# The output product's rows on two fixed sets of buffers, one of them lent by the prompt attention

## The chip, the cores and the metric

One core of a Trainium2 chip (trn2) runs the whole program. The metric is device time in microseconds (us) of one execution, taken as the median of several; lower is better. The engines are TensorE (PE; its weight loads are listed as PEld), VectorE (DVE), ScalarE (ACT), GpSimd (POOL) and SyncE (SP, which issues most DMAs, in order).

## The reference

One inference step of a small decoder with model width 1024: one recurrent layer (RG-LRU), from whose output shared keys, values and forget gates are made, then one attention layer with forget gates. It runs over 2048 prompt tokens and over 64 decode tokens (8 sequences of 8, each with 4096 cached keys). The change touches the end of the attention layer, its output product:

```python
def fox_mixer(x, k, v, cq, ck, q_pos, k_pos, w_in, w_out):
    z = x @ w_in
    q, g = z[..., :D_ATTN], z[..., D_ATTN:]
    o = fox_attention(q, k, v, cq, ck, q_pos, k_pos).reshape(B, T, D_ATTN)
    return (o * jax.nn.silu(g)) @ w_out

y = fox_mixer(rms_norm(x, b_pre_norm[l]), k_all, v_all, cq, ck, q_pos, k_pos, b_w_in[l], b_w_out[l])
x = x + rms_norm(y, b_post_norm[l])
```

All data are 32-bit floats. The kernel keeps that precision in products by splitting each factor into a high part, rounded to the format that PE takes, and a low part (the rest), and adding three products: high by high, high by low, low by high.

## The kernel before

The program first runs the recurrent layer, then the projections for keys, values, queries and gates, with the decode attention woven in. Last comes the prompt attention, and after it the output product with its norm and residual.

**Prompt attention** (`attention`, L1309 on). 64 units run one after the other: 16 heads by 4 blocks of 512 queries (`qc`). An odd head takes the blocks in the order 3, 2, 1, 0, so the last unit is head 15, block 0. Per unit, for each tile of 128 keys, PE makes scores into one of two banks of PSUM, the accumulator memory (`st`, L1537 to L1540), ACT takes the exponential into a tile `p` or, for the first, `acc` (L1546), PE multiplies groups of four with the values (`ops`, L1557), and POOL adds the exponentials up (`acc`, L1563). After a unit ACT copies the two halves of `ops` (`oT`, `odd`, L1438 and L1442) and POOL adds them; PE sums the exponentials (`tot`, L1460), ACT copies that (`cs`), small DMAs turn it round (`sums`, `r`), DVE takes the reciprocal, PE spreads it over the rows (`rp`, L1484), POOL and DVE multiply (`sgt`), and the gated result goes to a DRAM tensor per query block (`og_d[qc]`, L1487). These steps behind a unit are put off by some ticks in a list (`later`); `later.flush()` at the end of `attention` issues what is left.

The attention's keys and values lie in tiles of their own for even and odd heads: `kbs[0]`, `vvs[0]` and one of the two buffers tagged `ka` belong to the even heads, the last of which is head 14.

**Output product** (`project`, L1599). There are 17 rows of work (L1581): row 0 the 64 decode tokens, rows 1 to 16 blocks of 128 prompt tokens from the last block to the first, so rows 1 to 4 read `og_d[3]` and rows 13 to 16 `og_d[0]`. Per row: load 512 KB of gated attention (`og`) and 512 KB of residual (`x1`), cast the high part on ACT (`oh`, L99) and subtract for the low part on DVE (`ol`, L106), 2 x 24 matmuls of 128 x 512 into two banks (`y`, L368 to L370), then `post`: the sums of squares on ACT (`junk`, L499), a reciprocal square root of some twelve small operations on DVE (`nr_...`, L226 to L236), a scaling on DVE that reads the banks (`yo`, L1637), the residual added on POOL (L106), and the store.

The rows run in two groups. Rows 0 to 2 (`EARLY = 3`) use a pool `proje` with one buffer of each kind and two PSUM banks that the decode attention had (`psum["dec"]`, tags `d` and `o`). For rows 3 to 16 the attention's pools are closed, and a second pool, `proj`, with two buffers of each kind, and six PSUM banks (four of them for `y`) are opened on their memory.

The order of the instructions on each engine is not the order of the code: a scheduler takes, by its own estimates, the earliest instruction in the code that is ready, and places waits for data and for buffers. Each engine then runs its list in that order.

Of the kernel before, what the change touches and what calls it, by code (L numbers as in the profile page):

```python
# [11 lines left out]
F32 = mybir.dt.float32  # L12
F32R = mybir.dt.float32r
# [7 lines left out]
P = 128  # L21
D = 1024
KB = 8
SEQ = 2048
# [23 lines left out]
ODD = "G"  # L48
RAMP = 8
NS = 3  # L50
EARLY = 3
SHARE0 = 2.0
LEFT = 16
AHEAD = 8
# [25 lines left out]
def f(ap):  # L80

    return ap.bitcast(F32)
# [3 lines left out]
def tile_hawk_fox(  # L86
# [120 lines left out]
    def sbuf(es, name, side=None):  # L207
        return es.enter_context(tc.tile_pool(name=name, bufs=1, side=side, reuse_waits="tile"))

    def banks(es, name, n):  # L210
        return es.enter_context(tc.tile_pool(name=name, bufs=n, space=PSUM, reuse_waits="tile"))

    psum = {}

    def mmp(name="mm"):
        return psum["mm"].tile([P, 512], F32, name=name, tag="mm", bufs=4)
# [142 lines left out]
    later = Later()  # L359
# [629 lines left out]
    def drain(gen):  # L989
        for _ in gen:  # L990
            pass
# [317 lines left out]
    def attention(es):  # L1309
        pool = sbuf(es, "att")  # L1310
        ps3 = psum["att"]
# [8 lines left out]
        vvs = [pool.tile([P, 16, HD], F32, name=f"vvt{i}") for i in range(2)]  # L1320
        pool.tile([P, SEQ], F32R, name="ka", tag="ka", bufs=2)
        kbs = [pool.tile([P, SEQ], F32R, name="kbt0")]
# [30 lines left out]
               ident[:16, 8 + h2 * 4:12 + h2 * 4].unsqueeze(2).to_broadcast([16, 4, HD]), ALU.add)  # L1353
        less = pool.tile([4, 4], F32, name="less")
        V.tensor_scalar(less[:, :], ident[:4, :4], -1.0, 0.0, op0=ALU.mult, op1=ALU.add)
        units = [(h, qc) for h in range(H) for qc in ((0, 1, 2, 3) if h % 2 == 0 else (3, 2, 1, 0))]
        heads, qas, mxs, oTs_, sgt = {}, {}, {}, {}, {}

# [170 lines left out]
        for u, (h, qc) in enumerate(units):  # L1529
            load_low(u + 2)  # L1530
            for k in range(nks[u]):
# [44 lines left out]
                if k + sum(nks[u - u % 4:u]) == 3 and h + 1 < H:  # L1576
                    load_head(h + 1)
                yield 4.1 * (512 - lo) * 0.42 + (done[0] - before) * 213
        later.flush()

    rows = [(NSAMP, None, x1s_d[:, :], ys_flat)]  # L1581
    rows += [(P, t, x1_d[t:t + P], yp_flat[t:t + P]) for t in range(SEQ - P, -1, -P)]
    proj = {}
# [15 lines left out]
    def project(es):  # L1599

        bpostB, out = proj["g"], proj["out"]
        pool, nb = sbuf(es, "proje", "right"), 1
        raws, lds, xs = {}, {}, {}

        def load(i):
            if i >= lim:
                return
            m, t, res, _ = rows[i]
            og = pool.tile([P, KB, P], F32, name="ogT", tag="ogT", bufs=nb)
            if t is None:  # L1610
                tt(V, og[:, :, :m], oTs[:, :, :], sgs[:, :, :], ALU.mult)
            else:
                S.dma_start(og[:, :, :], og_d[t // 512][:, t % 512:t % 512 + P].rearrange("(k p) t -> p k t", p=P))
            x1 = pool.tile([P, D], F32, name="x1", tag="x1", bufs=nb)
            S.dma_start(x1[:m, :], res)
            raws[i], xs[i] = og, x1

        def split(i):
            if i >= lim:
                return  # L1620
            m = rows[i][0]
            og = raws.pop(i)
            oh = pool.tile([P, KB, P], F32R, name="ohT", tag="ohT", bufs=nb)
            ol = pool.tile([P, KB, P], F32R, name="olT", tag="olT", bufs=nb)
            cp(A, oh[:, :, :m], og[:, :, :m])
            tt(V, ol[:, :, :m], og[:, :, :m], f(oh[:, :, :m]), ALU.subtract)
            lds[i] = oh, ol

        def post(i, yps):
            m, t, res, dst = rows[i]  # L1630
            x1 = xs.pop(i)
            y = pool.tile([P, D], F32, name="yo", tag="yo", bufs=nb)
            ss = sumsq(pool, yps, m)
            r = rsqrt(ss[:m], m, 0.25 / D, post=0.5)
            for j in range(2):
                sl = slice(j * 512, (j + 1) * 512)
                V.scalar_tensor_tensor(y[:m, sl], yps[j][:m, :], r[:m, 0:1], bpostB[:m, sl], op0=ALU.mult, op1=ALU.mult)  # L1637
                tt(V if i == len(rows) - 1 and j == 1 else G, y[:m, sl], y[:m, sl], x1[:m, sl], ALU.add)
                if i == len(rows) - 1:
                    S.dma_start(dst[:, sl], y[:m, sl])  # L1640
            if i < len(rows) - 1:
                S.dma_start(dst, y[:m, :])

        for first, lim in ((0, EARLY), (EARLY, len(rows))):
            if first:
                yield
                pool, nb = sbuf(es, "proj"), 2
            for i in range(first, first + nb):
                load(i)
            split(first)  # L1650
            load(first + nb)
            for i in range(first, lim):
                yps = []
                for j in range(2):
                    ps = mmp("y") if first else psum["dec"].tile([P, 512], F32, name="y", tag="do"[j], bufs=1)
                    out.product(ps, rows[i][0], j, *lds[i])
                    yps.append(ps)
                    if j == 0 and nb > 1:
                        split(i + 1)
                post(i, yps)  # L1660
                if nb == 1:
                    split(i + 1)
                load(i + nb + 1)


    a_in = [[(0, a_w_in[0, :, n * P:(n + 1) * P]), (P, a_w_in[0, :, D + n * P:D + (n + 1) * P])] for n in range(KB)]
# [128 lines left out]
    psum["att"] = banks(att, "psa", 6)  # L1795
    side.along(attention(att), share)
    side.upto(1e12)
    pj = project(last)
    next(pj)
    att.close()  # L1800
    psum["mm"] = banks(last, "mm2", 6)
    drain(pj)
    last.close()


# [33 lines left out]
```

## Time and profile before

| | |
|---|---|
| median of 3 runs | 3090.72 us (3088.16 to 3099.72) |
| profiled execution, first to last instruction | 3081.2 us |
| mean granted clock of TensorE in it | 0.965 |
| PE busy | 2825.8 us (92%), 20462 instructions |
| DVE busy | 1805.6 us (59%) |
| ACT busy | 1295.0 us (42%) |
| POOL busy | 1155.5 us (38%) |
| first product of row 1 starts | 2864.39 us |
| last product of row 16 ends | 3071.80 us |

The profile is of one execution, and its times count from that execution's first instruction. A row of the timeline gives start, duration, engine, source line, operation, the tile written, the tiles read, shapes, count, and in brackets how long the engine had been idle and what ended the wait. SPq rows are DMA issues on SyncE's queue; what they show is the issue, not the transfer. A row of the busy times by stretch gives the stretch's start and end, its length, and then for each engine busy us with the number of instructions, the granted TensorE clock (1.00 is full), the busy share of the DMA engines and GB/s.

### The profile page before, as it was taken

What the parts mean: (1) busy time and instruction counts of PE and PEld (TensorE: products, weight loads), DVE (VectorE), ACT (ScalarE), POOL (GpSimd) and SP (SyncE); (2) the same over time, 40 slices, a digit from 0 to 9 for tenths busy, and PEclk for the clock granted to TensorE, in tenths of its full rate; (3) what the DMA queues carried; (4) which work ended last, traced back from release to release, by engine and by line L of the source; (5) the groups of instructions that cost most, each with busy time, mean ns of one, the idle gap of its engine ahead of it and who ended that gap; (6) DMA issues with size and microseconds to landing.
All of it is one profiled execution on the core that took longest, in us unless ns stands there. A gap on an engine that the chain in (4) does not pass through costs nothing.

```text
span 3081.2 us, 58151 instructions
## 1 busy us (share of the span) xinstructions
PE 2825.8 (92%) x20462; PEld 2177.5 (71%) x20462; DVE 1805.6 (59%) x4012; ACT 1295.0 (42%) x2874; POOL 1155.5 (38%) x1263
## 2 busy tenths in 40 slices
PE   6998999998999989997999799899999988999798
PEld 5997888988999978885797455455545554544587
DVE  7876555424367756755655666666667665543244
ACT  4665432232346655333333334444444445455211
POOL 1663101000025532000001456655656648788322
PEclk9999999999999999998999799999999999999899
DMA  4224547788622266999999998989999996331343
GB/s 121 89 76 150 154 137 216 242 267 254 198 84 86 79 195 198 327 305 315 325 331 307 292 303 261 289 268 321 289 294 314 317 295 211 97 87 41 96 135 111
DMA packets 492855, 653.25 MB, mean 212 GB/s; under 512 B 91100, under 2 KB 292829, under 8 KB 485286
## 3 DMA queue, kind: packets, MB, share of 16 engines
q1 hardware_dynamic: 488934, 643.87, 66.9%
q10 hardware_dynamic: 3340, 3.56, 0.4%
q8 instruction: 162, 2.65, 0.4%
q0 software_dynamic: 288, 2.10, 0.2%
q14 instruction: 131, 1.07, 0.1%
HBM read 513.82 MB, written 135.16 MB: 211 GB/s over the span
## 4 chain that ended last, share of the span: by engine, by line
PE 54%; DMA 20%; DVE 10%; ACT 5%; SPq 5%; issue 4%; POOL 2%; ACTq 0%; DVEq 0%; POOLq 0%
PE ops L1557 5%; DMA raw<-in_cache_k_dram 5%; PE y L368 4%; PE y L370 4%; PE y L369 4%; PE st L1537 3%; DMA raw<-in_cache_v_dram 3%; PE kv L369 3%; PE kv L368 3%; PE kv L370 3%; PE sx L1404 3%; PE dO L1237 2%; SPq L1074 2%; PE qg L368 2%; PE st L1538 2%
## 5 line engine op out<-in xcount | busy, mean ns | idle before, releaser
L106 POOL TENSOR_TENSOR acc<-acc,p 128x512 f32<-128x512 f32 (+3 forms) x576 | 638.8, 1109 | 291.7 <-PE ops L1557 226.4
L1546 ACT ACTIVATE p<-st 128x512 f32<-128x512 f32 (+3 forms) x576 | 290.4, 525 | 404.8 <-PE st L1538 188.6
L1159 DVE STREAM_TRANSPOSE ktr<-raw 128x1024 f32<-128x1024 f32 x256 | 305.4, 1223 | 161.3 <-DMA raw<-in_cache_k_dram 143.7
L1406 DVE TENSOR_REDUCE mxs<-sx 128x1 f32<-128x512 f32 x384 | 253.9, 680 | 143.5 <-PE sx L1404 142.5
L369 PE MATMUL kv<-wl,xh 128*128 128x256 f32 (+3 forms) x1088 | 309.1, 287 | 8.9 <-DVE wl L413 8.8
L368 PE MATMUL kv<-wh,xh 128*128 128x256 f32 (+3 forms) x1088 | 310.4, 290 | 5.7 <-ACT wh L412 5.3
L370 PE MATMUL kv<-wh,xl 128*128 128x256 f32 (+3 forms) x1088 | 309.2, 286 | 0.0
L1557 PE MATMUL ops<-p,vvt 128*64 128x512 f32 (+3 forms) x1152 | 292.7, 550 | 3.1 <-ACT p L1546 2.8
L1537 PE MATMUL st<-qa,ka 128*128 128x512 f32 (+3 forms) x640 | 273.3, 427 | 21.8 <-ACT p L1546 18.0
L1404 PE MATMUL sx<-kbt,qbt 96*128 96x512 f32 (+3 forms) x640 | 234.7, 426 | 26.1 <-DMA qbt<-qd 11.5
L1537 PEld LDWEIGHTS st<-qa,ka 128*128 128x128 f32 x640 | 123.6, 193 | 178.5 <-issue 112.1
L412 ACT ACTIVATE wh<-wst,gv 128x256 fp32r<-128x256 f32 (+1 forms) x384 | 164.4, 499 | 195.0 <-DMA wst<-in_b_w_in_dram 81.8
L1538 PE MATMUL st<-qbt,kbt 128*128 128x512 f32 (+3 forms) x640 | 237.0, 371 | 0.0
L413 DVE SCALAR_TENSOR_TENSOR wl<-wst,gv,wh 128x256 fp32r<-128x256 f32 (+1 forms) x384 | 169.9, 492 | 108.1 <-ACT wh L412 100.3
L368 PE MATMUL qg<-xh,wh 128*128 128x384 f32 (+2 forms) x640 | 229.1, 359 | 1.0 <-ACT wh L412 1.0
L370 PE MATMUL qg<-xh,wl 128*128 128x384 f32 (+2 forms) x640 | 227.5, 357 | 0.9 <-DVE wl L413 0.9
L369 PE MATMUL qg<-xl,wh 128*128 128x512 f32 (+2 forms) x640 | 226.9, 356 | 0.0
L1092 POOL TENSOR_TENSOR qw<-qb,amask 128x128 f32<-128x128 f32 x64 | 29.3, 465 | 498.8 <-PE dS L1127 258.0
L369 PEld LDWEIGHTS kv<-wl,xh 128*128 128x128 f32 (+1 forms) x1088 | 203.8, 188 | 12.7 <-DVE wl L413 10.4
L368 PEld LDWEIGHTS kv<-wh,xh 128*128 128x128 f32 (+1 forms) x1088 | 203.6, 189 | 11.8 <-ACT wh L412 6.0
L370 PEld LDWEIGHTS kv<-wh,xl 128*128 128x128 f32 (+1 forms) x1088 | 205.3, 189 | 3.9 <-issue 3.9
L1404 PEld LDWEIGHTS sx<-kbt,qbt 96*128 96x128 f32 x640 | 119.1, 203 | 94.4 <-DVE mxs L1406 25.1
(289 smaller groups left out, 6472.1 us busy)
## 6 DMA issues: line engine op xcount, KB each, us to landing
raw<-in_cache_k_dram SPq DMA_DIRECT2D x512, 256.0 KB
raw<-in_cache_v_dram SPq DMA_DIRECT2D x512, 256.0 KB
wst<-in_w_kv_dram SPq DMA_DIRECT2D x48, 512.0 KB
wst<-in_b_w_in_dram SPq DMA_DIRECT2D x48, 512.0 KB
xt<-in_x_prompt_dram SPq DMA_DIRECT2D x32, 512.0 KB
wst<-in_a_w_in_dram SPq DMA_DIRECT2D x64, 256.0 KB
x<-x SPq DMA_DIRECT2D x32, 512.0 KB
out_dram<-kf SPq DMA_DIRECT2D x128, 128.0 KB
```

Of the source, the lines that this page charges most:

```text
L106: eng.tensor_tensor(out, a, b, op=op)
L368: T.matmul(ps, lh(k), rh(k), start=(k == 0), stop=False)
L369: T.matmul(ps, lh(k), rl(k), start=False, stop=False)
L370: T.matmul(ps, ll(k), rh(k), start=False, stop=(k == nk - 1))
L413: V.scalar_tensor_tensor(wl[:, k, :], st[:, k, :], gk, f(wh[:, k, :]), op0=ALU.mult, op1=ALU.subtract)
L1159: V.transpose(t.kts[pp][:, n], raw[:, :, pp * 256:(pp + 1) * 256])
L1404: T.matmul(ps[:, :w], qb[0:96, j * P:(j + 1) * P], kb[0:96, ck * 512:ck * 512 + w], start=True, stop=True)
L1406: V.reduce_max(mx[:, j, ck:ck + 1], ps[:, :w], axis=AX.X)
L1537: T.matmul(ps[:, lo:], ka[:, ks], qa[:, lo:], start=True, stop=False)
L1538: T.matmul(ps[:, lo:], kb[:, ks], qb[:, lo:], start=False, stop=(k < qc * 4))
L1546: pair.append((k, lo, p, A.activation(p[:, lo:], ps[:, lo:], AF.Exp)))
L1557: return T.matmul(ops[r:r + HD, lo:], vvs[h % 2][:, k, :], p[:, lo:], start=(k < 2), stop=(last and k >= todo[-1][0] - 1))
```

## The change

Rows 0 to 16 all use two fixed sets of buffers in turn, row i the set i % 2. Set 0 is the pool `proje` and the two decode banks. Set 1 is lent by the attention through a dictionary: `og` and `x1` are the two halves of `kbs[0]`, `oh` and `ol` the two halves of a further tile with the tag `ka`, `y` is `vvs[0]`, and its PSUM banks are two further tiles with the tag `st`. The second pool and the six banks are gone. A row's load of `og` for row i + 2 and the split of row i + 1 are written behind the first half of row i's products, the load of the residual for row i + 2 behind row i's `post`. `later.flush()` moves from the end of `attention` to behind row 3. Lines of the changed kernel are up to two lower or higher than those of the kernel before; the operations themselves are the same.

```diff
--- before.py
+++ after.py
@@ -48,7 +48,6 @@
 ODD = "G"
 RAMP = 8
 NS = 3
-EARLY = 3
 SHARE0 = 2.0
 LEFT = 16
 AHEAD = 8
@@ -1353,6 +1352,8 @@
                ident[:16, 8 + h2 * 4:12 + h2 * 4].unsqueeze(2).to_broadcast([16, 4, HD]), ALU.add)
         less = pool.tile([4, 4], F32, name="less")
         V.tensor_scalar(less[:, :], ident[:4, :4], -1.0, 0.0, op0=ALU.mult, op1=ALU.add)
+        lent["psum"], lent["res"], lent["out"] = ps3, f(kbs[0][:, :]), vvs[0]
+        lent["halves"] = lambda: pool.tile([P, SEQ], F32R, name="ka", tag="ka", bufs=2)
         units = [(h, qc) for h in range(H) for qc in ((0, 1, 2, 3) if h % 2 == 0 else (3, 2, 1, 0))]
         heads, qas, mxs, oTs_, sgt = {}, {}, {}, {}, {}
 
@@ -1576,7 +1577,8 @@
                 if k + sum(nks[u - u % 4:u]) == 3 and h + 1 < H:
                     load_head(h + 1)
                 yield 4.1 * (512 - lo) * 0.42 + (done[0] - before) * 213
-        later.flush()
+
+    lent = {}
 
     rows = [(NSAMP, None, x1s_d[:, :], ys_flat)]
     rows += [(P, t, x1_d[t:t + P], yp_flat[t:t + P]) for t in range(SEQ - P, -1, -P)]
@@ -1599,37 +1601,28 @@
     def project(es):
 
         bpostB, out = proj["g"], proj["out"]
-        pool, nb = sbuf(es, "proje", "right"), 1
-        raws, lds, xs = {}, {}, {}
-
-        def load(i):
-            if i >= lim:
-                return
+
+        def tiled(t):
+            return t.rearrange("p (k t) -> p k t", k=KB)
+
+        def gated_rows(i, og):
             m, t, res, _ = rows[i]
-            og = pool.tile([P, KB, P], F32, name="ogT", tag="ogT", bufs=nb)
             if t is None:
                 tt(V, og[:, :, :m], oTs[:, :, :], sgs[:, :, :], ALU.mult)
             else:
                 S.dma_start(og[:, :, :], og_d[t // 512][:, t % 512:t % 512 + P].rearrange("(k p) t -> p k t", p=P))
-            x1 = pool.tile([P, D], F32, name="x1", tag="x1", bufs=nb)
+
+        def residual(i, x1):
+            m, t, res, _ = rows[i]
             S.dma_start(x1[:m, :], res)
-            raws[i], xs[i] = og, x1
-
-        def split(i):
-            if i >= lim:
-                return
+
+        def split(i, og, oh, ol):
             m = rows[i][0]
-            og = raws.pop(i)
-            oh = pool.tile([P, KB, P], F32R, name="ohT", tag="ohT", bufs=nb)
-            ol = pool.tile([P, KB, P], F32R, name="olT", tag="olT", bufs=nb)
             cp(A, oh[:, :, :m], og[:, :, :m])
             tt(V, ol[:, :, :m], og[:, :, :m], f(oh[:, :, :m]), ALU.subtract)
-            lds[i] = oh, ol
-
-        def post(i, yps):
+
+        def post(i, pool, yps, x1, y):
             m, t, res, dst = rows[i]
-            x1 = xs.pop(i)
-            y = pool.tile([P, D], F32, name="yo", tag="yo", bufs=nb)
             ss = sumsq(pool, yps, m)
             r = rsqrt(ss[:m], m, 0.25 / D, post=0.5)
             for j in range(2):
@@ -1641,26 +1634,38 @@
             if i < len(rows) - 1:
                 S.dma_start(dst, y[:m, :])
 
-        for first, lim in ((0, EARLY), (EARLY, len(rows))):
-            if first:
-                yield
-                pool, nb = sbuf(es, "proj"), 2
-            for i in range(first, first + nb):
-                load(i)
-            split(first)
-            load(first + nb)
-            for i in range(first, lim):
-                yps = []
-                for j in range(2):
-                    ps = mmp("y") if first else psum["dec"].tile([P, 512], F32, name="y", tag="do"[j], bufs=1)
-                    out.product(ps, rows[i][0], j, *lds[i])
-                    yps.append(ps)
-                    if j == 0 and nb > 1:
-                        split(i + 1)
-                post(i, yps)
-                if nb == 1:
-                    split(i + 1)
-                load(i + nb + 1)
+        pool = sbuf(es, "proje", "right")
+        hs = lent["halves"]()
+        sets = [dict(og=pool.tile([P, KB, P], F32, name="ogT"), x1=pool.tile([P, D], F32, name="x1"),
+                     oh=pool.tile([P, KB, P], F32R, name="ohT"), ol=pool.tile([P, KB, P], F32R, name="olT"),
+                     y=pool.tile([P, D], F32, name="yo"),
+                     ps=lambda j: psum["dec"].tile([P, 512], F32, name="y", tag="do"[j], bufs=1)),
+                dict(og=tiled(lent["res"][:, :D]), x1=lent["res"][:, D:], oh=tiled(hs[:, :D]), ol=tiled(hs[:, D:]),
+                     y=lent["out"][:, :, :].rearrange("p k d -> p (k d)"),
+                     ps=lambda j: lent["psum"].tile([P, 512], F32, name="y", tag="st", bufs=2))]
+
+        def part(i, fn, *names):
+            if i < len(rows):
+                fn(i, *(sets[i % 2][n] for n in names))
+
+        for i in range(2):
+            part(i, gated_rows, "og")
+            part(i, residual, "x1")
+        part(0, split, "og", "oh", "ol")
+        for i in range(len(rows)):
+            b = sets[i % 2]
+            yps = []
+            for j in range(2):
+                ps = b["ps"](j)
+                out.product(ps, rows[i][0], j, b["oh"], b["ol"])
+                yps.append(ps)
+                if j == 0:
+                    part(i + 2, gated_rows, "og")
+                    part(i + 1, split, "og", "oh", "ol")
+            post(i, pool, yps, b["x1"], b["y"])
+            part(i + 2, residual, "x1")
+            if i == 3:
+                later.flush()
 
 
     a_in = [[(0, a_w_in[0, :, n * P:(n + 1) * P]), (P, a_w_in[0, :, D + n * P:D + (n + 1) * P])] for n in range(KB)]
@@ -1795,11 +1800,8 @@
     psum["att"] = banks(att, "psa", 6)
     side.along(attention(att), share)
     side.upto(1e12)
-    pj = project(last)
-    next(pj)
+    project(last)
     att.close()
-    psum["mm"] = banks(last, "mm2", 6)
-    drain(pj)
     last.close()
 
 
```

## The prediction

> **What bounds the kernel now.** I read the page, then the chain of waits from 2830 us on, then the timeline, and last the busy times by stretch. The order of instructions does not differ before the last head of the attention, so only the end counts. Rows of the output product are numbered as the code numbers them: row 0 the decode tokens, row 1 tokens 1920 to 2047, row 16 tokens 0 to 127. TensorE (PE) sets the end: it multiplies until 3071.80 us, and 9.40 us of work on the last row follow. This is PE's time from the first product of row 1 on, cut where it stands or slows:
>
> ```profile
> core 0: us, PE busy (x) PEld busy (x) DVE busy (x) ACT busy (x) POOL busy (x), PEclk, DMA share, GB/s
> 2864.39:2884.29 19.90, 18.05 (x80) 11.97 (x80) 4.26 (x8) 7.76 (x17) 10.14 (x9) 1.00 0.13 41
> 2884.29:2885.80 1.51, 1.50 (x8) 0.70 (x8) 1.34 (x6) 0.00 (x0) 0.36 (x1) 1.00 0.14 45
> 2885.80:2891.30 5.50, 0.00 (x1) 0.01 (x1) 5.18 (x11) 1.05 (x2) 4.02 (x5) 0.73 0.12 38
> 2891.30:2895.42 4.12, 4.12 (x7) 1.67 (x8) 0.60 (x1) 0.00 (x0) 2.51 (x2) 0.53 0.15 24
> 2895.42:2905.93 10.51, 10.51 (x46) 8.37 (x45) 0.83 (x4) 1.64 (x4) 0.00 (x0) 1.00 0.23 91
> 2905.93:2912.81 6.88, 0.01 (x2) 0.00 (x1) 4.55 (x17) 1.36 (x3) 2.46 (x2) 0.71 0.80 260
> 2912.81:2915.84 3.03, 3.03 (x7) 2.41 (x8) 1.20 (x1) 0.94 (x1) 0.03 (x1) 0.53 1.10 373
> 2915.84:3071.80 155.96, 155.95 (x666) 125.05 (x664) 60.07 (x195) 30.05 (x67) 33.02 (x26) 1.00 0.43 127
> 3071.80:3081.20 9.40, 0.00 (x0) 0.00 (x0) 4.67 (x15) 0.69 (x2) 1.26 (x1) 0.73 0.15 56
> ```
>
> Rows 3 to 16 run without a pause: of their 14 x 48 = 672 products all but the first seven take 155.96 us, 0.2345 each at full clock, 11.3 us a row. PE stands for 5.50 and 6.88 us, and each time the next stretch has a clock of 0.53. These rows say why:
>
> ```profile
> 2884.29 0.64 PE L1557 MATMUL ops<-acc,vvt 128*64 128x512 f32 x1 [1.54 <-ACT p L1546]
> 2885.16 0.16 DVE L106 TENSOR_TENSOR ss<-sq 128x1 f32<-128x1 f32 x1
> 2885.44 1.79 POOL L106 TENSOR_TENSOR acc<-acc,p 128x384 f32<-128x384 f32 x2 [4.14 <-PE ops L1557]
> 2887.32 0.99 POOL L106 TENSOR_TENSOR oT<-oT,odd 64x384 f32<-64x384 f32 x1
> 2888.79 1.26 POOL L106 TENSOR_TENSOR sgt<-sgt,oT 128x512 f32<-128x512 f32 x1
> 2888.89 1.18 DVE L230 SCALAR_TENSOR_TENSOR nr_t<-nr_y,nr_m 128x1 f32<-128x1 f32 x1
> 2890.49 1.41 DVE L1637 SCALAR_TENSOR_TENSOR yo<-y,nr_y,bpostB 128x512 f32<-128x512 f32 x2
> 2891.30 0.80 PE L368 MATMUL y<-woh,ohT 128*128 128x512 f32 x1 [5.50 <-DVE yo L1637]
> 2906.51 0.92 SPq L1487 DMA_DIRECT2D ogd<-sgt  x2
> 2907.48 0.45 SPq L1613 DMA_DIRECT2D ogT<-ogd  x1
> 2911.71 1.04 ACT L99 CAST ohT<-ogT 128x1024 fp32r<-128x1024 f32 x1 [5.46 <-DMA ogT<-ogd]
> 2912.81 0.79 PE L368 MATMUL y<-woh,ohT 128*128 128x512 f32 x1 [6.87 <-ACT ohT L99]
> 2914.89 1.05 ACT L99 CAST ohT<-ogT 128x1024 fp32r<-128x1024 f32 x1 [2.14 <-DMA ogT<-ogd]
> ```
>
> The first stop: row 2 needs the two accumulator banks of row 1, which come free when VectorE (DVE) writes row 1's result (yo). The second: rows from 3 on live in a pool opened over the attention's memory, so their first load goes out only at 2907.48, behind the last gated tile (2906.51); 4.2 us of DMA and a 1.04 us cast follow.
>
> **What the change removes.** (1) The pause of 1.54 us at 2884.29, where PE waits for the exponential of the last unit: row 1's products (48 x 0.2345 = 11.3 us) now stand there. On PE, where the last scores of the attention end, before:
>
> ```order
> L1538 MATMUL st<-qbt_19541,kbt_19545 128x128
> L1540 LDWEIGHTS identB
> L1540 MATMUL st<-causal,identB 128x128
> L1557 MATMUL ops<-acc,vvt_19535 64x512
> L1557 MATMUL ops<-p,vvt_19535 64x384
> L1557 MATMUL ops<-p,vvt_19535 64x256
> L1557 MATMUL ops<-p,vvt_19535 64x128
> L368 MATMUL y<-woh_33180,ohT 128x512
> ```
>
> In the change 48 products from the lent set (ka) follow those scores directly; they are row 1, and row 2 (ohT) has gone ahead of it. At their end stands:
>
> ```order
> L369 MATMUL y<-woh_33175,ka 128x512
> L1558 MATMUL ops<-acc,vvt_19535 64x512
> L1558 MATMUL ops<-p,vvt_19535 64x384
> L1558 MATMUL ops<-p,vvt_19535 64x256
> L1558 MATMUL ops<-p,vvt_19535 64x128
> L1461 MATMUL tot<-acc,ones 32x512
> L367 MATMUL y<-woh_33135,ka 128x512
> ```
>
> The last row is row 3, on the lent set again; after it the sets alternate: 4, 5, 6. (2) The stop of 5.50 us: row 1 takes the attention's two score banks, not those of row 2. (3) The slow clock behind it: 4.12 us hold 5 products and one total (two records, 1.04 us at 2869.39, below), 5 x 0.2345 + 1.04 = 2.21, so 1.91 are lost. (4) The stop of 6.88 us: rows 3 and 4 load as soon as rows 1 and 2 are split. (5) The slow clock behind that: 7 products in 3.03 instead of 1.64, 1.39. Sum: 1.54 + 5.50 + 1.91 + 6.88 + 1.39 = 17.22 us.
>
> **What it adds.** Term a, the start. On ScalarE (ACT), where the first rows are cast (p<-st is an exponential of the attention, ohT<-ogT the cast of a row in its own tiles, ka<-kbt that of one in the lent tiles), before:
>
> ```order
> L1438 COPY oT<-ops 64x512
> L1442 COPY odd<-ops 64x512
> L1546 ACTIVATE p<-st 128x512 x2
> L99 CAST ohT<-ogT 128x1024
> L1546 ACTIVATE p<-st 128x512
> ```
>
> and in the change:
>
> ```order
> L1439 COPY oT<-ops 64x512
> L1443 COPY odd<-ops 64x512
> L1547 ACTIVATE p<-st 128x512
> L98 CAST ka<-kbt_19537 128x1024
> L1547 ACTIVATE p<-st 128x512
> L98 CAST ohT<-ogT 128x1024
> ```
>
> Row 1's cast has moved ahead of an exponential, and row 2's stands behind it.
>
> ```profile
> 2858.11 0.43 SPq L1613 DMA_DIRECT2D ogT<-ogd  x1
> 2859.97 1.09 ACT L1546 ACTIVATE p<-st 128x512 f32<-128x512 f32 x2
> 2863.30 1.05 ACT L99 CAST ohT<-ogT 128x1024 fp32r<-128x1024 f32 x1 [2.23 <-DMA ogT<-ogd]
> 2864.39 0.50 PE L368 MATMUL y<-woh,ohT 128*128 128x512 f32 x1 [0.49 <-ACT ohT L99]
> 2866.17 0.36 SPq L1613 DMA_DIRECT2D ogT<-ogd  x1
> 2869.39 1.04 PE L1460 MATMUL tot<-acc,ones 128*32 128x512 f32 x2
> 2871.08 0.56 SPq L1467 DMA_DIRECT2D sums<-cs  x1
> 2875.79 1.50 PE L1557 MATMUL ops<-p,vvt 128*64 128x512 f32 x8
> ```
>
> The cast waits for its load until 2863.30 in both. Now one exponential (1.09 / 2 = 0.55) waits behind it, and for that exponential one attention product (four instructions, 1.50 us, which used to fill PE while the load came); then row 2's cast (1.05). PE's first output product comes 1.05 + 0.55 + 1.50 = 3.1 us later. Low: 1.6, if only ACT's part counts. High: 4.7, if the second load of the pair lands late as at 2907.48 (casts at 2911.71 and 2914.89, 3.2 apart, where 1.6 are covered).
>
> Term b, rows 1 and 3 on one set. Row 3 needs the score banks, which come free when DVE scales row 1. On DVE row 2's norm (sq_33408) is woven into row 1's (it writes vvt):
>
> ```order
> L105 TENSOR_TENSOR ss<-sq_33408 128x1
> L229 SCALAR_TENSOR_TENSOR nr_t<-nr_y,nr_m 128x1
> L225 TENSOR_SCALAR nr_m<-ss 128x1
> L233 TENSOR_SCALAR nr_t<-nr_t 128x1
> L226 TENSOR_SCALAR nr_y<-nr_m 128x1
> L105 TENSOR_TENSOR nr_y<-nr_y,nr_t 128x1
> L229 SCALAR_TENSOR_TENSOR nr_t<-nr_y,nr_m 128x1 x2
> L233 TENSOR_SCALAR nr_t<-nr_t 128x1 x2
> L105 TENSOR_TENSOR nr_y<-nr_y,nr_t 128x1
> L235 SCALAR_TENSOR_TENSOR nr_y<-nr_y,nr_t 128x1
> L229 SCALAR_TENSOR_TENSOR nr_t<-nr_y,nr_m 128x1
> L1630 SCALAR_TENSOR_TENSOR vvt_19534<-y,nr_y,bpostB 128x512 x2
> ```
>
> So row 1 waits for row 2's sums, the last of which stands on ACT behind row 3's cast, two sums and the two copies of the last unit.
>
> ```profile
> 2883.38 0.60 ACT L499 ACTIVATE junk<-y 128x512 bf16<-128x512 f32 x1
> 2883.87 0.19 ACT L499 ACTIVATION_READ_ACCUMULATOR junk<-y 128x1 f32 x1
> 2885.84 0.58 ACT L1438 COPY oT<-ops 64x512 f32<-64x512 f32 x1 [1.61 <-PE ops L1557]
> 2886.45 0.47 ACT L1442 COPY odd<-ops 64x384 f32<-64x384 f32 x1
> 3071.89 0.60 ACT L499 ACTIVATE junk<-y 128x512 bf16<-128x512 f32 x1 [4.95 <-PE y L370]
> 3072.61 0.16 DVE L106 TENSOR_TENSOR ss<-sq 128x1 f32<-128x1 f32 x1 [7.29 <-ACT junk L499]
> 3075.14 1.41 DVE L1637 SCALAR_TENSOR_TENSOR yo<-y,nr_y,bpostB 128x512 f32<-128x512 f32 x2
> ```
>
> From row 1's end: cast 1.05, two sums 2 x 0.79, copies 1.05, third sum 0.79 = 4.5 us. Then the first row above and 12 small operations; undisturbed, the 12 from 3072.61 to 3075.14 take 2.5, so 13 take 2.7. Half of 1.41 frees the first bank: 4.5 + 2.7 + 0.7 = 7.9, with hops between engines about 8.1. PE has 1.50 + 1.04 = 2.5 of work in it: a stop of 5.6 in all, the low end. High: GpSimd (POOL) works meanwhile, and DVE's operations with two inputs wait for it: 2888.89 took 1.18 and ended with POOL's 2888.79; that chain took 2890.49 - 2885.16 = 5.3 instead of 2.5. So up to 2.8 more, 8.4. I take 6.2: of POOL's four operations there only the 1.26 one (sgt) falls late enough to delay, on average by half.
>
> Term c, the clock after this stop: 1.39 to 1.91 were lost after stops of 5.50 and 6.88; I take 1.7, low 0, high 1.9. The Trainium skill ("TensorE: Matmul & The Clock Gate", section "Part 1: The HAM clock gate") says that the clock halves after an idle window of about 3.4 us, which does not start with the kernel's own pause. The 0.53 behind both stops agrees. The total would cut the new stop into two of some 2 and 4 us; by that rule either could happen, and the sum without c would be 1.7 us lower.
>
> Hidden: the lent tiles belong to the even heads, idle since head 14 ended, so no load waits for them, and row 1's residual, which now goes out ahead of the last row sums on SP's queue, holds nothing up (a load that is late all the same adds its delay to a); rows 4 to 16 have 11.3 us between two uses of a set, against an undisturbed 3071.80 to 3075.85 = 4.1 from a row's end to its bank. The last two gated tiles are written while row 4 runs and read from row 9 on, some four rows or 45 us later. The end on row 16 is the same, 9.40.
>
> **Sum.** 3.1 + 6.2 + 1.7 = 11.0 added against 17.22 removed: 6.2 us less. With the bounds, 1.6 + 5.6 + 0 = 7.2 or 4.7 + 8.4 + 1.9 = 15.0 added, it is 10.0 or 2.2 less. The profiled span of 3081.2 becomes 3075.0; the median of the runs, 3090.72, stands 9.5 above that span, so I forecast 3084.5.
>
> **Rivals.**
>
> Full relief: DVE frees the score banks in time, b and c vanish and a is 1.6. Gain 17.22 - 1.6 = 15.6, 3075.1. For it: 11.3 us separate the uses of a set everywhere else. Against: the order puts rows 1 and 3 next to each other.
>
> No gain: on SP's queue the loads of rows 3 and 4 now both wait for DVE's split (before, one did, until 2866.17) ahead of the small DMA of the next row sums, and so of the total's way back to PE. That one went out at 2871.08; with a, row 2's cast ends near 2866.0 and its split some 1.3 us later, so 3.7 us are left. Every us beyond costs one, and a split 9.9 us later takes the whole gain: 3090.7. Against: the landings seen differ by 3.2 us at most.
>
> Slower: a set has one accumulator pair, one result, one residual; where row i's way to its bank takes longer than row i + 1 on PE, every row waits. Price: 13 rows x (way - 11.3); from 11.8 on it eats the gain, at 13.0 it costs 22.1, 15.9 more than the gain, so 3106.6. For it: POOL doubled DVE's chain once. Against: 4.1 us undisturbed, and POOL is busy 33.02 of 155.96 us there.
>
> **How the numbers follow.** Forecast 0.62, full relief 0.18, no gain 0.13, slower 0.07. About 0.5% (15.5 us) is what a measurement of this kernel can tell from no change. Full relief lies at that bound, and the runs shown spread over 3088.16 to 3099.72: faster by more 0.22, within 0.71, slower by more 0.07. The forecast's own range is 3080.7 to 3088.4; with full relief below and the runs' spread above, 3074 to 3095.
>
> **What would show it.** Right: row 2's first product near 2867.5; no pause before the last attention products; one stop of about 6 us in two pieces between rows 1 and 3, ended by DVE's vvt; none from row 4 on. Wrong: no such stop (full relief), a first product later than 2869 (a), or a wait for DVE or a DMA that returns with every row.

## The result and the profile after

| | before | change |
|---|---|---|
| median of the runs, us | 3088.16 (11 runs, 3082.91 to 3099.72) | 3073.72 (11 runs, 3067.60 to 3082.32) |
| ratio, 95% interval | | 0.9964 (0.995 to 0.9978) |
| span of the profiled execution, us | 3081.2 | 3071.8 |
| from the score named below to PE's last product, us | 215.24 | 205.65 |

By the ratio the gain is 0.36%, less than 0.5%, and its interval stays below 1 (the two medians alone would give 0.9953). The forecast was 3084.5 from a span of 3075.0. The span came out 3.2 us lower than that, and the median 10.8 lower. By the ratio, the 3090.72 us that the forecast started from become 3079.6: 1.1 below its own range (3080.7 to 3088.4), inside the wide one (3074 to 3095). The median of the runs lies 0.3 below the wide one.

The last line of the table needs a word. The time ahead of the last head differs between executions: one and the same score of the attention, the one that waits 0.69 us for ACT's `acc`, starts between 2850.58 and 2862.58 us in the profiles of this study. So the traces are compared from that score on; single times and spans are not. In the kernel before, the timeline has it here (start, duration, instruction, the idle time before it and what ended that):

```profile
2856.55 0.50 PE L1537 MATMUL st<-qa,ka 128*128 128x512 f32 x1 [0.69 <-ACT acc L1546]
```

The timeline of the change, with the same score first, then the start of the output product, then the stop between rows 1 and 3:

```profile
2856.70 0.50 PE L1538 MATMUL st<-qa,ka 128*128 128x512 f32 x1 [0.69 <-ACT acc L1547]
...
2862.30 1.04 ACT L98 CAST ka<-kbt 128x1024 fp32r<-128x1024 f32 x1 [1.60 <-DMA kbt<-ogd]
2863.25 0.59 ACT L1547 ACTIVATE p<-st 128x512 f32<-128x512 f32 x1
2863.89 0.87 PE L1558 MATMUL ops<-acc,vvt 128*64 128x512 f32 x1 [2.34 <-ACT p L1547]
2867.90 0.48 PE L367 MATMUL y<-woh,ohT 128*128 128x512 f32 x1
...
2896.72 1.04 ACT L98 CAST ka<-kbt 128x1024 fp32r<-128x1024 f32 x1 [4.70 <-PE y L368]
2898.07 3.14 POOL L105 TENSOR_TENSOR acc<-acc,p 128x384 f32<-128x384 f32 x3 [13.83 <-PE ops L1558]
2901.15 0.15 DVE L105 TENSOR_TENSOR ss<-sq 128x1 f32<-128x1 f32 x1
2901.26 1.04 DVE L229 SCALAR_TENSOR_TENSOR nr_t<-nr_y,nr_m 128x1 f32<-128x1 f32 x1
2901.26 1.49 PE L1461 MATMUL tot<-acc,ones 128*32 128x512 f32 x2 [2.91 <-POOL acc L105]
2901.29 0.99 POOL L105 TENSOR_TENSOR oT<-oT,odd 64x384 f32<-64x384 f32 x1
2902.36 1.26 POOL L105 TENSOR_TENSOR sgt<-sgt,oT 128x512 f32<-128x512 f32 x1
2902.52 1.12 DVE L105 TENSOR_TENSOR nr_y<-nr_y,nr_t 128x1 f32<-128x1 f32 x1
2904.33 1.40 DVE L1630 SCALAR_TENSOR_TENSOR vvt<-y,nr_y,bpostB 128x512 f32<-128x512 f32 x2
2905.22 0.77 PE L367 MATMUL y<-woh,ka 128*128 128x512 f32 x1 [2.46 <-DVE vvt L1630]
```

And its busy times by stretch, as in the prediction; the last two lines are one row of the output product each, row 8 on the own set and row 9 on the lent one:

```profile
core 0: us, PE busy (x) PEld busy (x) DVE busy (x) ACT busy (x) POOL busy (x), PEclk, DMA share, GB/s
2863.89:2867.90 4.01, 4.01 (x12) 1.17 (x12) 1.94 (x2) 1.54 (x2) 3.15 (x3) 0.57 0.44 133
2867.90:2885.40 17.50, 17.50 (x81) 12.09 (x81) 2.12 (x7) 5.04 (x11) 8.28 (x8) 1.00 0.16 51
2885.40:2896.85 11.45, 11.45 (x51) 8.98 (x51) 1.34 (x2) 1.94 (x5) 0.00 (x0) 1.00 0.22 64
2896.85:2898.35 1.50, 1.50 (x9) 0.71 (x8) 0.55 (x1) 1.50 (x3) 0.28 (x1) 1.00 0.00 0
2898.35:2905.22 6.87, 1.50 (x4) 0.17 (x3) 6.70 (x22) 3.01 (x8) 5.03 (x6) 0.75 0.26 77
2905.22:2908.34 3.12, 3.12 (x8) 2.47 (x8) 3.05 (x10) 0.00 (x0) 2.45 (x2) 0.50 0.01 1
2908.34:3062.35 154.01, 154.01 (x668) 125.30 (x666) 61.23 (x198) 29.94 (x66) 35.56 (x28) 1.00 0.42 137
2962.80:2973.68 10.88, 10.88 (x49) 9.01 (x48) 4.61 (x15) 2.31 (x6) 2.54 (x2) 1.00 0.45 143
2973.68:2984.92 11.24, 11.24 (x49) 9.04 (x48) 4.61 (x15) 2.33 (x6) 2.54 (x2) 1.00 0.45 149
```

Three things are to be seen. Row 1 stands where the pause before the last attention products was (2885.40 to 2896.85, no gap), and behind 2908.34 PE never stops. Between rows 1 and 3 it stops twice, 2.91 us for POOL's sum and 2.46 us for DVE's `vvt`. And a row takes 10.88 us on the own set and 11.24 on the lent one, at the full clock, with the same work on every other engine: 48 products at 0.2267 us against 0.2342 (the expectations below have 0.2270 and 0.2343 for the same two paces). The last was not in the forecast. The kernel before has both paces too: 33 products of row 2 (first pool) take 7.48 us, 0.2267 each, and row 7, as every row of the second pool, takes 11.25, 0.234 each:

```profile
2897.59:2905.07 7.48, 7.48 (x34) 6.19 (x33) 0.69 (x3) 0.69 (x2) 0.00 (x0) 1.00 0.18 71
2959.17:2970.42 11.25, 11.25 (x50) 9.04 (x48) 4.62 (x15) 2.33 (x6) 2.54 (x2) 1.00 0.48 138
```

### The profile page after: what moved, and what is told of

It is laid out like the page before. It is cut to its first block, busy times and chain, and to the rows that moved or that the text cites. A ratio compares the mean times of both kernels' runs of the same rounds, so it can differ in the third digit from the quotient of the medians.

```text
span 3071.8 us, 58144 instructions
## 1 busy us (share of the span) xinstructions
PE 2826.8 (92%) x20462; PEld 2178.9 (71%) x20462; DVE 1805.2 (59%) x4012; ACT 1294.9 (42%) x2874; POOL 1158.7 (38%) x1263
## 4 chain that ended last, share of the span: by engine, by line
PE 56%; DMA 18%; DVE 10%; ACT 6%; SPq 5%; issue 4%; POOL 2%; DVEq 0%; ACTq 0%; POOLq 0%
PE ops L1558 6%; DMA raw<-in_cache_k_dram 4%; PE y L367 4%; PE y L368 4%; PE y L369 4%; PE st L1538 4%; DMA raw<-in_cache_v_dram 4%; PE sx L1405 3%; PE kv L369 3%; PE kv L367 3%; PE kv L368 3%; PE dO L1236 3%; PE st L1539 3%; PE dS L1126 2%; PE qg L367 2%
```

## The experiments

In all of them "score to last product" is the measure named above: 215.24 us before, 205.65 in the change. Where a time is compared with the kernel before, its interval is given; the other figures are from one execution each. In e3, e8, e10 and e11, whose start is the same, PE's pause at the start was 2.20, 1.85, 2.01 and 1.94 us, so a few tenths of a microsecond on this measure say nothing.

**e1, the turn of the sets exchanged.** Rows 1, 3, 5 ... on the own set, rows 2, 4, 6 ... on the lent one, so that no two neighbours on PE share a set. Rows 0 and 1 then share the own set, so row 1 is loaded behind row 0's split.

```diff
+        def at(i):
+            return sets[(i + 1) % 2 if i else 0]
...
-                fn(i, *(sets[i % 2][n] for n in names))
+                fn(i, *(at(i)[n] for n in names))
...
-            b = sets[i % 2]
+            b = at(i)
...
-                if j == 0:
+                if j == 0 and i:
...
+            if not i:
+                part(1, split, "og", "oh", "ol")
             post(i, pool, yps, b["x1"], b["y"])
-            part(i + 2, residual, "x1")
+            part(i + 2 if i else 1, residual, "x1")
```

> Rows 0 and 1 on the own set, row 2 on the lent set, row 3 on the own one, and so on: PE takes the rows in the order 1, 2, 3, 4, and no two neighbours share a set. Theory (the stop between rows 1 and 3 is made by the set that they share, the late start by row 1's cast standing ahead of row 2's): the stop of 5.9 us, the 1.5 lost at the slow clock behind it and the 3.5 at the start all go, 10.9 together; the profiled span falls from 3071.8 to about 3061, no idle stretch of PE over 1 us is left between 2870 and 3060 us, and row 1's first product is near 2864.4 as before the change. Rival (DVE's woven norms make the wait, whichever set the rows are on): the stop returns one row later, at row 3 or 4, and the span stays within 1 us of 3071.8. Second rival (the pace of a row, not the stop, decides): 8 rows on the lent set in both, so no change either.

Measured: ratio to before 0.995 (0.9935 to 0.9966), span 3063.6, score to last product 198.49: 7.2 us less than the change, not 10.9. Its timeline and two stretches:

```profile
2861.79 0.49 PE L367 MATMUL y<-woh,ohT 128*128 128x512 f32 x1 [1.21 <-ACT ohT L98]
2884.48 0.51 PE L367 MATMUL y<-woh,ka 128*128 128x512 f32 x1 [0.71 <-ACT p L1547]
```

```profile
2861.79:2865.79 4.00, 4.00 (x10) 1.58 (x12) 3.25 (x2) 1.99 (x3) 2.50 (x3) 0.57 0.27 86
2895.75:2920.82 25.07, 25.07 (x109) 18.82 (x108) 12.06 (x30) 6.36 (x14) 10.33 (x9) 1.00 0.36 117
```

Row 3 and the attention's last products follow row 2 with PE busy throughout, at the full clock: terms b and c of the prediction are gone, and the stop did not return one row later. The third part of the theory, the late start, failed. Row 1's cast is still ahead of an exponential on ACT; PE still pauses, 1.21 us, and the clock behind is 0.57. A pause of 0.71 us is new: row 2's first product waits for a score bank.

**e3, row 3 on other banks.** One line; the turn is that of the change, so row 3 shares its tiles with row 1, but not the accumulators.

```diff
-                ps = b["ps"](j)
+                ps = b["ps"](j) if i != 3 else lent["psum"].tile([P, 512], F32, name="y", tag="sx", bufs=3)
```

> Row 3 alone takes two of the three other score banks of the attention (sx), all else as in the changed kernel. Theory (row 3 waits for row 1's accumulator banks, not for its tiles): row 3 follows the last attention products after at most 0.3 us, the total stands behind row 3 in the order, and of 5.9 + 1.5 nothing is left: span 3071.8 - 7.4 = 3064.4, the start of the rows still late (first output product near 2867.9). Rival (the shared tiles: row 3's cast must wait for row 1's last product): the cast at 2896.7 + 1.04 us would end before the attention products do (2898.35), so a wait for it would be below 0.5 us; were it longer, the row is ended by ACT's cast and the span falls by less than 7. Rival (DVE is the bottleneck and the stop is only handed on): row 4 or 5 stops by about 5.9 and the span stays near 3071.8.

Measured: ratio 0.9932 (0.9911 to 0.9954), span 3062.2, score to last product 198.29, 7.4 us less than the change. The start is as before this edit, and behind row 1 nothing waits:

```profile
2861.51 1.07 PE L1558 MATMUL ops<-acc,vvt 128*64 128x512 f32 x1 [2.20 <-ACT p L1547]
```

```profile
2883.10:2908.30 25.20, 25.20 (x108) 18.71 (x107) 12.74 (x32) 7.56 (x17) 9.50 (x9) 1.00 0.25 75
```

So the stop was a wait for banks and not for the tiles, and nothing was handed on to rows 4 or 5. Its price, 5.37 us idle, 0.46 on the total and 1.48 on the products behind (7.3 together), is what came back.

**e4, the flush put back to the attention's end.**

```diff
                 yield 4.1 * (512 - lo) * 0.42 + (done[0] - before) * 213
+        later.flush()
...
-            if i == 3:
-                later.flush()
```

> The flush of the attention's last steps (row sums, totals and the gated tiles) goes back to the end of the attention, so they stand ahead of row 3 in the order instead of beside rows 1 to 3. Theory (the gain is in the two sets, and the flush's place is worth little): the stop between rows 1 and 3 stays; the total and the last attention products no longer lie in it, so it is 6 to 8 us instead of 5.9, and 1.5 to 2.5 us of work have moved out of it; span 3071.8 to 3074. Rival (the flush's place carries the gain): 3077 or more.

Measured: span 3073.6, score to last product 207.55, 1.9 us more than the change. The stop between rows 1 and 3 is still there, 5.89 us, with less work inside it:

```profile
2907.02 1.19 PE L1485 MATMUL rp<-r,sel 128*128 128x512 f32 x2 [5.89 <-DVE vvt L1631]
```

By this execution the flush's place is worth at most some 1.9 of the change's 9.6 us, and the sets make most of the gain. Even the 1.9 is not all the flush's: in this execution the clock was at 0.50 for 6.83 us at the start (2865.97 to 2872.80) instead of 3.41, and whether the flush or chance did that was not tested. PE's pauses are only 0.6 us longer in all than in the change.

**e5, the kernel before with one part alone: row 2 on the score banks.**

```diff
-                    ps = mmp("y") if first else psum["dec"].tile([P, 512], F32, name="y", tag="do"[j], bufs=1)
+                    ps = mmp("y") if first else psum["dec"].tile([P, 512], F32, name="y", tag="do"[j], bufs=1) if i < 2 else \
+                        psum["att"].tile([P, 512], F32, name="y", tag="st", bufs=2)
```

> The kernel before, with one part of the change alone: row 2 takes the attention's two score banks instead of row 1's; the one early set of tiles and the second pool stay. Theory (the stop of 5.50 us was a wait for banks, the one of 6.88 us comes from the second pool): row 2 follows row 1 after its own cast, some 1.6 us instead of 5.50, without the 1.91 us of slow clock; row 3 still stops for 6 to 7 us plus its slow clock, and that stop comes 4 to 6 us earlier, since the last gated tile waits for row sums that stand behind row 2 on PE. Span 3081.2 - 4 to 6 = 3075 to 3077. Rival (the second pool's load is tied to the attention's end, which does not move): the second stop grows by what the first one loses, to 11 to 13 us, and the span stays within 1 us of 3081.

Measured: span 3082.8, score to last product 213.86, only 1.4 us less than before. The theory fell. The rival held in kind: the second stop grew, to 12.33 us in two pieces.

```profile
2886.35 0.50 PE L368 MATMUL y<-woh,ohT 128*128 128x512 f32 x1 [0.66 <-ACT ohT L99]
2905.88 1.19 PE L1484 MATMUL rp<-r,sel 128*128 128x512 f32 x2 [5.29 <-DMA r<-rs]
2914.12 0.80 PE L368 MATMUL y<-woh,ohT 128*128 128x512 f32 x1 [7.04 <-ACT ohT L99]
```

The 5.50 us before row 2 became 0.66, as expected, but PE then stood 5.29 us for the last row sums (a DMA) and 7.04 for the second pool's first load. The chain of total, row sums, last gated tile and load runs at its own pace; a row that is done earlier only waits longer for it. The two stops of the kernel before had the same end, and removing one alone moved its time into the other.

**e2, the banks of the two sets swapped from row 6 on**, the first of four runs on the pace.

```diff
-                ps = b["ps"](j)
+                ps = sets[(i + (i >= 6)) % 2]["ps"](j)
```

> From row 6 on the two sets exchange their accumulator banks and keep their tiles: even rows have the own tiles and the attention's score banks, odd rows the lent tiles and the decode banks. It is to tell why a product starts every 0.2270 us on one set and every 0.2343 on the other. If the banks set the pace: even rows from 6 on go at 0.2343 and odd ones at 0.2270. If the place of the stationary tiles sets it: even rows stay at 0.2270 and odd ones at 0.2343. The span is no test here: rows 5 and 6 share the score banks, so one stop of 4 to 6 us and some 1.5 us of slow clock are added, 3071.8 + 5.5 to 7.5 = 3077 to 3079.

Measured: span 3079.2. Row 9 (lent tiles, decode banks) and row 10 (own tiles, score banks) by stretch:

```profile
2981.15:2992.39 11.24, 11.24 (x49) 9.04 (x48) 4.61 (x15) 2.33 (x6) 2.54 (x2) 1.00 0.36 112
2992.39:3003.28 10.89, 10.89 (x50) 9.01 (x48) 4.61 (x15) 2.32 (x6) 2.54 (x2) 1.00 0.41 135
```

The pace stays with the tiles and not with the banks. The stop that sharing banks makes came with the swap, as in term b: 4.59 us before the next row on those banks.

**e8, e10 and e11, the tiles moved by a few bytes.** All three are e3 with padding. In e8 every own tile moves by 32 bytes; in e10 and e11 `ka` moves by 32 and 160 bytes, and the padding behind it leaves the other lent tiles at whole multiples of 64 bytes from where they were. Of the tiles that move, PE's output products read `ohT` and `olT` in e8 and `ka` in the others. The program places the own `ohT` at byte 146400 of each partition, the lent `ka` at 72256, the weights `woh0` at 163808, and in the kernel before the second pool's `ohT` at 43584 and 47680. Every slice that PE takes from these tiles starts a multiple of 512 bytes further.

```diff
 e8:
+        pool.tile([P, 8], F32, name="pad")
+
         def part(i, fn, *names):
 e10:
+        pool.tile([P, 8], F32, name="pada")
         pool.tile([P, SEQ], F32R, name="ka", tag="ka", bufs=2)
+        pool.tile([P, 8], F32, name="padb")
 e11: as e10, with 40 numbers ahead and 8 behind
```

> The kernel with row 3 on other banks (e3), and 32 bytes of padding at the end of the own pool, which moves the own tiles from byte 146400 to 146368 of each partition: out of step with a 64-byte grid by 32 before, on it now, as the lent tiles are (72256). If the start of the stationary tile within 64 bytes sets the pace: even rows go at 0.2343 us a product instead of 0.2270, as the odd ones do, and the rows take 8 x 48 x 0.0073 = 2.8 us more. If the region of the memory sets it (own tiles above 138000, lent ones below 89000): no change, 0.2270 and 0.2343.

> The counterpart: the kernel with row 3 on other banks (e3), with the attention's tiles ka alone moved by 32 bytes (72256 to 72288), all other lent tiles where they were to within whole 64 bytes, the order of all instructions the same. If the start within 64 bytes sets the pace: the rows on the lent set go at 0.2270 too, and all rows together take 2.8 us less than in e3 (198.3 to 195.5 from the score at 2854.45 to the last product). If the region sets it: no change.

> As e10, but the tiles ka are moved by 160 bytes instead of 32 (72416, which leaves 224 over whole 256 bytes, as the own tiles at 146400 and the weights at 163808 do; 72288 left 96). e8 and e10 showed that the start of the stationary tile sets the pace (0.2343 on the 64-byte grid), but 72288 gave 0.2317, not the 0.2270 of the own tiles. If the start within 256 bytes counts: rows on ka go at 0.2270, and score to last product falls from the 198.3 us of e3 to 195.5. If 32 off the 64-byte grid is all that counts there, and the rest is the region: 0.2317 again and 197.4 us, as in e10.

Measured, one row each by stretch: e8's row 8 on the own tiles, e10's row 9 on `ka`, e11's row 9 on `ka`:

```profile
2959.35:2970.55 11.20, 11.20 (x50) 9.00 (x49) 4.61 (x15) 2.33 (x6) 2.55 (x2) 1.00 0.47 151
```

```profile
2961.04:2972.20 11.16, 11.16 (x50) 9.04 (x48) 4.61 (x15) 2.33 (x6) 2.55 (x2) 1.00 0.46 149
```

```profile
2958.40:2969.28 10.88, 10.88 (x50) 9.01 (x48) 4.61 (x15) 2.32 (x6) 2.54 (x2) 1.00 0.45 145
```

| tile | start | over whole 256 bytes | us a product (a row by 48) | score to last product |
|---|---|---|---|---|
| own, e3 | 146400 | 224 | 0.2267 | 198.29 |
| own, e8 | 146368 | 192 | 0.2333 | 200.17 |
| `ka`, e3 | 72256 | 64 | 0.2342 | 198.29 |
| `ka`, e10 | 72288 | 96 | 0.2325 | 197.39 |
| `ka`, e11 | 72416 | 224 | 0.2267 | 195.02 |

The region of the memory is out: the own tiles become slow by 32 bytes, `ka` fast by 160. e10 was between, which neither theory had foreseen, and e11 was made for it. By the rows, eight of them cost 2.6 us more in e8 and save 0.6 in e10 and 2.9 in e11; the measured ends differ from e3's by 1.9, 0.9 and 3.3, each a few tenths off as the start allows. The second pool of the kernel before (43584 and 47680, both 64) fits the slow rows.

**e7, e12 and e14, the late start.** e7 is e3 with the casts of rows 1 and 2 on DVE, e12 is e1 with row 1's alone there, e14 is e11 with row 1's alone there.

```diff
-            cp(A, oh[:, :, :m], og[:, :, :m])
+            cp(V if i in (1, 2) else A, oh[:, :, :m], og[:, :, :m])
 e12 and e14:
+            cp(V if i == 1 else A, oh[:, :, :m], og[:, :, :m])
```

> The kernel with row 3 on other banks (e3), and the casts of rows 1 and 2 on DVE instead of ACT. It is to settle the late start, which the exchanged turn (e1) did not remove. Theory (term a: a cast on ACT ahead of an exponential holds the attention's product, and the pause makes the clock slow): PE's pause of 2.20 us before that product falls below 1 us, the 4.09 us at a clock of 0.58 behind it shrink by 1.5 or more, and from the score at 2854.45 to the last product it is 194.5 to 196.5 us instead of 198.3. Rival (the loads set the start, not ACT): the pause moves to the first output product and the stretch stays within 0.7 us of 198.3.

> The exchanged turn (e1), and row 1's cast alone on DVE. Now the first row that PE multiplies is also the first that is cast, and ACT has no cast ahead of the exponential. Theory (the late start is a cast on the path of the exponential, plus the slow clock that its pause brings; e7 failed because row 1's split stood ahead of row 2's cast on DVE): no pause over 0.85 us at the start, the clock in the 4 us behind it at 0.9 or more instead of 0.6, and from the score at 2855.73 to the last product 196 to 197 us instead of the 198.5 of e1. Rival (the load's landing sets the start, whichever engine casts): within 0.7 us of 198.5.

> Row 3 on other banks and ka moved by 160 bytes (e11), and row 1's cast alone on DVE, so that ACT's order at the start is that of the kernel before: two exponentials, then row 2's cast. Theory (term a is made by a second split at the start: any engine that does row 1's work ahead of what PE needs next makes PE pause about 2 us, and the clock is slow behind it; e1, e7 and e12 each left one such piece in the way): the attention products start without a pause, row 2's first product waits at most 1 us, the clock behind stays at 0.9 or more, and from the score at 2850.58 to the last product it is 195.0 - 1.5 to 3 = 192 to 193.5 us. Rival (the landing of row 2's load, one transfer behind row 1's, sets the start): a pause of 1.5 us or more before row 2's first product, with the slow clock, and 194.3 to 195.5 us. Against the kernel before (215.2 us) the ratio is 0.993 by either within the error.

Measured: e7 198.06 and e12 198.66 us, where 194.5 to 197 were expected; e14 192.59, as expected. In e7 the attention's products started at once, but row 2's cast stood behind row 1's subtraction on DVE:

```profile
2863.63 2.18 DVE L105 TENSOR_TENSOR ka<-kbt,ka 128x1024 fp32r<-128x1024 f32 x1
2866.73 0.50 PE L367 MATMUL y<-woh,ohT 128*128 128x512 f32 x1 [1.95 <-DVE ohT L102]
```

In e12 the first four products stood ahead of the attention's on PE, and waited for their cast (1.35 us, then a clock of 0.57). Both are pieces of the same kind in another place, so "the cast ahead of the exponential" was too narrow. By their times alone both runs came out as their rival had it (the load's landing sets the start); e14 decides between the two, and there PE neither pauses for 1.5 us nor gets the slow clock, as that rival would have it:

```profile
2869.68 1.04 ACT L98 CAST ohT<-ogT 128x1024 fp32r<-128x1024 f32 x1 [2.60 <-DMA ogT<-ogd]
2870.78 0.50 PE L367 MATMUL y<-woh,ohT 128*128 128x512 f32 x1 [0.85 <-ACT ohT L98]
```

```profile
2866.64:2870.78 4.14, 3.29 (x15) 1.28 (x15) 2.93 (x2) 1.54 (x3) 4.06 (x4) 1.00 0.78 236
2870.78:2888.30 17.52, 17.52 (x80) 12.14 (x80) 4.35 (x9) 5.52 (x12) 11.34 (x10) 1.00 0.26 80
2900.79:3055.17 154.38, 154.38 (x677) 126.53 (x676) 72.53 (x228) 32.94 (x75) 43.23 (x35) 1.00 0.43 140
```

Row 1's cast and subtraction are on DVE, and PE waits for nothing of DVE there; row 2's product waits 0.85 us for its cast, and the clock stays at 1.00. The cast itself waits for its load, so the 0.85 us that are left of the late start (0.49 in the kernel before) are the load's.

**e13, the exchanged turn, row 1's cast on DVE and `ka` moved by 160 bytes**: e12 (which holds e1) with the padding of e11; row 3 keeps the banks of its set.

> Both: the exchanged turn, row 1's cast on DVE, and the tiles ka moved by 160 bytes. The sum of the two theories: 196.5 - 2.8 = 193.7 us from the score to the last product (before: 3071.79 - 2856.55 = 215.2; the change: 205.7), so a span of 3059.7 and a ratio to the kernel before of 0.993. If ka goes on at 0.2317 and the start is not mended, 197.5 us and 3063.5.

Measured: ratio 0.9931 (0.9905 to 0.9957), span 3062.7, score to last product 195.87: 2.8 us below e12, whose order of instructions is the same, so the pace came as expected. The start did not: PE pauses for 1.40 us before its first output product, and the sum is 2.2 us above the 193.7 expected.

The versions that were timed stand at 0.995 (e1), 0.9932 (e3), 0.9931 (e13) and 0.9947 (0.9925 to 0.9968, e14). Their intervals overlap. By the traces e14 has the shortest end, 22.6 us less than before; its times do not show it apart from e3, since executions differ by 12 us ahead of the score. All four lie below the change's 0.9964 (0.995 to 0.9978); the intervals of e3 and of the change still touch, at 0.995 to 0.9954, so that e3 beats the change rests on the traces (7.4 us) with the times in agreement.

## Why the prediction was right, and where its size was off

The mechanism held at the stops that were named. The size was short: 6.2 us of gain were forecast, and from the score to the last product it is 9.6, within the bounds of 2.2 to 10.0. One term of the sum was missing, and one came out near its forecast by luck.

- **What is removed, 17.22.** All five pieces are gone from the trace. e5 shows how far they can be added: only together. Terms 2 and 3 alone, 7.41 by the prediction, were worth 1.4 in that run, because the chain behind the fourth set the end of both.
- **Term a, 3.1 forecast (1.6 to 4.7), 3.4 measured**: from the score to the first output product it is 11.20 us after and 7.84 before. It was composed otherwise than thought: 1.85 us more of idling (2.34 against 0.49) and some 1.7 of slow clock (4.01 us at 0.57); the forecast had only delays in it. It also took the first cast to wait for its load as long as before; the cast in fact started 5.60 us behind the score instead of 6.75. The slow clock and the earlier cast nearly cancel, so that 3.4 is near 3.1 is luck. The cause was right in kind, a second row's split at the start: without row 1's cast on ACT (e14) both are gone but for 0.85 us of waiting.
- **Term b, 6.2 forecast, 5.8 measured**: 2.91 + 2.46 idle and 0.46 on a total that took 1.50 instead of 1.04. DVE's chain was held by POOL as assumed, twice (1.04 beside `oT`, 1.12 beside `sgt`) and not once. From row 2's sums (2901.15) to `vvt` (2904.33) it took 3.18 us against the 2.7 reckoned undisturbed, 0.5 more, where 0.6 had been allowed. e3 shows that the wait was for the banks.
- **Term c, 1.7 forecast, 1.5 measured**: seven products in 3.12 us instead of 1.64, at a clock of 0.50.
- **The sum.** Added 3.4 + 5.8 + 1.5 = 10.7 against 11.0: the change should have given 17.22 - 10.7 = 6.5 us, and the trace gives 9.6.
- **The step that failed: "Rows 3 to 16 run without a pause: ... 0.2345 each at full clock, 11.3 a row."** That was read as the price of any row, and the change of tiles was put at nothing. It is the price of a row in the tiles of the second pool. The change takes those tiles away: 8 of the 16 rows now run in the own tiles, where before 2 did, and 6 x (11.24 - 10.88) = 2.2 us are gained with no wait involved. e8 and e11 show that the tile's start does this. The kernel before had it in plain sight in row 2, which went at 0.2267, but the prediction priced rows 3 to 16 alone. Of the 0.9 us that are left, 0.30 is a short pause of the kernel before that the sum leaves out and the change does not have; the rest is not traced:

```profile
2866.20 0.50 PE L370 MATMUL y<-woh,olT 128*128 128x512 f32 x1 [0.30 <-DVE olT L106]
```

- **The median.** The forecast put the median 9.5 us above the profiled span, from three runs. The change's profiled execution took 3073.57 with a span of 3071.8, so 1.8 us are fixed; the rest was the scatter of executions. Over 11 runs the median before fell to 3088.16.
- **The rivals.** Full relief did not happen in the change. e3 has the part on terms b and c, and e14 that on the start too, for the reason given: 11 us separate two uses of the banks once rows 1 and 3 do not share them. Some of the 16.9 and 22.6 us that they gain is the pace. No wait on SP's queue took the gain. The slow turn did not come: behind 2908.34 PE is busy 154.01 of 154.01 us.

Of the clock, the Trainium skill ("TensorE: Matmul & The Clock Gate", section "Part 1: The HAM clock gate") says that it halves after an idle window of about 3.4 us. The traces differ here: behind a pause of 2.34 us the granted clock was 0.57, and in e1 behind one of 1.21 us, with 0.79 some 2 us earlier; behind 0.85 us in e14 it was 1.00. In the kernel before, the clock was still 1.00 for 4.08 us (2884.29 to 2888.37) behind a pause of 1.54 us, so the length of the last pause alone does not tell.

## What to carry to other kernels

Two stops that end in one chain are not two gains: look for what the second waits for before adding them, and try one part alone. When buffers are used in turn, look at the order in which the engine takes the work, not at the index: the scheduler put row 2 ahead of row 1, so rows 1 and 3 were neighbours on one set; one other pair of banks for one row gave 7.4 us in the trace. And a row's price belongs to its tiles: when a change moves operands, compare the product's pace on the old and the new place before multiplying.

## What the runs showed of the hardware

The pace of a 128x512 product in fp32r, the format that PE takes here, depends on where its stationary tile (`oh` or `ol`, which PE loads ahead of the product) starts: 0.2267 us at 224 over whole 256 bytes, 0.2325 at 96, 0.2333 at 192, 0.2342 at 64. Whether 224 is good in itself, or because the weights `woh` start at 224 too (163808), was not tried; no other start was. The moving side, the banks and the region of the memory were the same or made no difference.

Pauses of PE that are well below 3 us can already bring a slow clock behind them: 1.21 us in e1, 1.35 in e12, 2.34 in the change, each with about 4 us at 0.57. In these three the clock was at 0.50 for 3.41 or 3.42 us, from 0.48, 0.48 and 0.29 us after the products had set in again. Pauses seem to add up: in the 3.41 us before the clock fell, PE had stood for 2.34 us in the change, for 2.00 in e1 and for 2.14 in e12, in two pauses each in the last two. One of 1.54 us in the kernel before was not enough, nor were 0.77 and 0.85 us in e14, which lie 4.1 us apart. Where the limit lies was not tested.
